# Splitting 512-column TensorE products into two of 256 in six dense stages of a hybrid block, with shifted weight tiles, seven more start-up products and two more K buffers

## Chip, cores and metric

The kernel runs on one core of a Trainium2 chip. The metric is the device time of one execution in microseconds; three executions of the kernel before the change are shown with their median. The engines have short names: PE is TensorE (matrix products), PEld its weight loads, DVE is VectorE, ACT is ScalarE, POOL is GpSimd, SP is SyncE, which here issues transfers.

## What is computed

One layer of a streaming encoder on 512 tokens of width 1024, in fp32. Two token mixers run side by side on one input projection and are gated and added, then come cross-attention into a memory of 256 rows and a gated FFN with a short convolution. Cut to what matters here:

```python
h = rms_norm(x, norm_mix_g)
proj = h @ w_in + b_in                    # 1024 -> 4864: stage "in"
y_a = rwkv7_branch(proj[..., :cb0], ...) @ w_branch_a          # stage "ya"
y_b = rglru_branch(proj[..., cb0:cb1], proj[..., cb1:cb2], ...) @ w_branch_b   # "yb"
merged = sigmoid(proj[..., cb2:cg1]) * y_a + sigmoid(proj[..., cg1:]) * y_b
x = x + merged @ w_mix_out                # "mix"
# cross-attention: keys and values of the memory, "k" and "v"
q = rms_norm(x, norm_x_g) @ w_cq          # "q"
x = x + attention(q, mem @ w_ckv) @ w_co  # "co"
x = x + conv_ffn(rms_norm(x, norm_ffn_g), w_ffn_in, ..., w_ffn_out)
return rms_norm(x, norm_final_g)
# rwkv7_branch: S_t = S_{t-1} diag(w_t) + (S_{t-1} a_t) b_t^T + v_t k_t^T, y_t = S_t r_t
```

## The kernel before

Activations are held transposed: 128 channels on the partitions, the 512 tokens along the free dimension. A dense stage goes through its output in blocks of 128 channels; each block is one accumulator `ps` of 128 x 512 in PSUM, and its sum runs over blocks of 128 input channels.

Every fp32 operand is split into a high and a low half of a shorter type (fp32r), and a product of fp32 matrices is three products of halves: `mm3` makes high by high (L179), high weight by low activation (L180) and low weight by high activation (L181). `dense` (L201 to L209) calls `mm3` for each input block and takes the weights from a `Units` object, which streams them from HBM: SP loads 128 x 1024 of raw weights (512 KB, L112), ACT casts them to the high half (L122), DVE subtracts for the low half (L123). The high half lies in a tile that `weight_tiles` allots; its argument `at` says how many elements from the tile's start the data begins. OFF is 32 elements, 128 bytes. Before the change the K, V and FFN stages pass OFF, the six stages named in, yb, ya, mix, q and co pass nothing and start at 0. K and FFN products have 256 columns, those of the six stages 512. An optional `nsum` lets `dense` put small products of a running sum (`sum_behind`) behind one of its own.

The stages run in this order. First `wake`: NWAKE products of constants (L300) on PE while the first weights arrive. Then the K stage: eight accumulators `k_ps` of 256 columns, each scaled by DVE into a tile `kt` (L360) and stored by POOL to the scratch `dK` (L361); `kt` has six buffers. Then V (`v_ps`), then the input projection: 38 blocks `in_ps`, in an order written out at the head of the file: 12, 13, 4, 5, 0, 1, 8, 9, 6, 7, 2, 3, 10, 11 and then 22 to 37, 14 to 21. Each block is 8 input blocks by 3 products. Its result is scaled by ACT and mixed with the token before by DVE (L597, L598); these make `pr` (r), `pk` (k) and `vT` (v) of the delta-rule branch, whose four pairs of heads, 0 to 3, are prepared while the projection goes on. For a pair i, PE makes two small products `psw` and `psa` (L620, L621), a sum of squares `ss`, and 16 small products `sc` (L691, from `AK` and `KBt`); DVE makes `KBt` from `kk` and `pk` (L653, L654) and evacuates `sc` into `AK` and `BZ` (L696, L697), ACT copies parts of `BZ` (L698). Of all pairs, SP stores a matrix (`dM`) and loads it again in another layout (`Nm`); on it DVE runs a serial chain of 32 steps (`zz` and `Zt`, L763 and L764), copied to `Zn`. The recurrence over chunks follows (products `zh`, `zo` and others) amid the last blocks of the projection, then yb, ya, mix, q with the attention, co, the FFN and the output.

What sets the order: each engine runs its instructions in one fixed order and waits at each for semaphores of other engines. The order is made by the tile framework's scheduler when the kernel is built, from priorities, dependences and its own costs; a change of the number or the size of instructions so moves others, too. Buffers of a tile name are used in turn, and an instruction that writes a buffer waits for the readers of what lay in it before: `in_ps` blocks so wait for the DVE instruction that read an earlier block.

Of the kernel before, what the change touches and what calls it, by code (L numbers as in the profile page):

```python
# [9 lines left out]
F32 = mybir.dt.float32  # L10
# [7 lines left out]
P = 128  # L18
T = 512
D = 1024  # L20
KB = D // P
NMEM = 256
# [11 lines left out]
NMID = 10  # L34
NWAKE = 11
KNORM = 5
# [22 lines left out]
def hybrid_block_kernel(ctx: ExitStack, tc: tile.TileContext, xT_d, mT_d, pv_d, cst_d, win_d, wk_d, wv_d,  # L59
# [39 lines left out]
    OFF = 32  # L99
# [78 lines left out]
    def mm3(ps, lh, ll, rh, rl, start, stop, **kw):  # L178
        first = PE.matmul(ps, lh, rh, start=start, stop=False, **kw)  # L179
        PE.matmul(ps, lh, rl, start=False, stop=False, **kw)  # L180
        PE.matmul(ps, ll, rh, start=False, stop=stop, **kw)  # L181
        return first
# [18 lines left out]
    def dense(ps, units, rhs, nkb, nsum=0):  # L201

        for kb in range(nkb):
            wh, wl = units.next()
            rh, rl = rhs(kb)
            ins = mm3(ps, wh, wl, rh, rl, kb == 0, kb == nkb - 1)
            if kb * nsum % nkb < nsum:
                sum_behind(ins)
        return ins  # L209
# [85 lines left out]
    with tc.tile_pool(name="p0", bufs=1, reuse_waits="tile") as p0:  # L295
# [6 lines left out]
        o = PV["nmem"][0]  # L302
# [55 lines left out]
        def k_out(m):  # L358
            kt = p0.tile([P, NMEM], F32, tag="kt", name=f"kt{m}", bufs=6)
            ins = V.tensor_tensor(kt, k_ps[m], rm, ALU.mult)  # L360
            nc.gpsimd.dma_start(dK[m], kt)  # L361
            return ins
# [36 lines left out]
        for hf in range(2):  # L399
            pss = [(mm_ps if hf else rw_ps)(f"v_ps{hf}_{i}") for i in range(2)]  # L400
            for k2 in range(4):
                wh, wl = next(st)
                for kk in range(2):
                    kb = 2 * k2 + kk
                    rh, rl = wh[:, kk * T:(kk + 1) * T], wl[:, kk * T:(kk + 1) * T]
# [170 lines left out]
    for i in range(2):  # L576
        with tc.issue_after(wdma[-1].ins):
            nc.sync.dma_start(lraw[i], lup_d[i])
    uin = Units(win_d, "win")
    last_in = None  # L580
# [131 lines left out]
    for jp in range(2):  # L712
# [10 lines left out]
        for j in js:  # L723
# [3 lines left out]
            at, L, Pp = prep(j)  # L727
# [22 lines left out]
    with tc.tile_pool(name="pz", bufs=1, reuse_waits="tile") as pz:  # L750
# [9 lines left out]
        for s in range(30, -1, -1):  # L760
            n = 31 - s
# [245 lines left out]
    for b in range(4):  # L1007
        yb = YB[:, b, :]
        with tc.high_priority():
            S.copy(yb2[:, 0, b, :], yb)  # L1010
            V.tensor_tensor(yb2[:, 1, b, :], yb, yb2[:, 0, b, :].bitcast(F32), ALU.subtract)
    ub = Units(wbb_d, "wbb")
    for m in range(KB):
# [11 lines left out]
    pm = pm_ctx.enter_context(tc.tile_pool(name="pm", bufs=2, reuse_waits="tile"))  # L1025
    ua = Units(wba_d, "wba")
    for m in range(KB):
# [25 lines left out]

    um = Units(wmix_d, "wmix")
    for m in range(KB):
        xin = pm.tile([P, T], F32, tag="xin", name=f"xin{m}")
        nc.scalar.dma_start(xin, xT_d[:, m, :])
        ps = mm_ps(f"mix_ps{m}")
# [57 lines left out]
    vs = vs[1:] + load_kv("V", 1)  # L1116
    uq = Units(wq_d, "wq")

# [78 lines left out]
    order = [0, 4, 1, 5, 2, 6, 3, 7]  # L1197
    uo = Units(wo_d, "wo", order)
    for m in order:
        ps = mm_ps(f"co_ps{m}")  # L1200
# [367 lines left out]
```

## Time and profile before

| | |
|---|---|
| time, median of three (lowest, highest) | 880.66 us (880.45, 881.25) |
| the profiled execution's own time | 880.43 us |
| its span, first to last instruction | 878.6 us |
| mean granted clock of TensorE | 0.997 |
| in_ps7, first and last product start | 108.02, 113.28 us |
| in_ps22, first product start | 147.21 us |
| in_ps14, first product start | 245.53 us |
| yb, first product start | 345.41 us |

The span is what the profile covers; the metric has 1.8 us more. Starts are counted from the span's first instruction. In the profile's rows numbers of buffers are left out, so `in_ps` stands for all 38 blocks; which one a row belongs to follows from its place in the order above, 24 products to a block. The duration printed for a product includes its way through the array, and products overlap: the distance between two starts is what one costs.

### The profile page before, as it was taken

What the parts mean: (1) busy time and instruction counts of PE and PEld (TensorE: products, weight loads), DVE (VectorE), ACT (ScalarE), POOL (GpSimd) and SP (SyncE); (2) the same over time, 40 slices, a digit from 0 to 9 for tenths busy, and PEclk for the clock granted to TensorE, in tenths of its full rate; (3) what the DMA queues carried; (4) which work ended last, traced back from release to release, by engine and by line L of the source; (5) the groups of instructions that cost most, each with busy time, mean ns of one, the idle gap of its engine ahead of it and who ended that gap; (6) DMA issues with size and microseconds to landing.
All of it is one profiled execution on the core that took longest, in us unless ns stands there. A gap on an engine that the chain in (4) does not pass through costs nothing.

```text
span 878.6 us, 15940 instructions
## 1 busy us (share of the span) xinstructions
PE 864.2 (98%) x6197; PEld 754.2 (86%) x6197; DVE 676.5 (77%) x1096; ACT 514.6 (59%) x788; POOL 132.6 (15%) x163
## 2 busy tenths in 40 slices
PE   8999999999999999999999999999999999999996
PEld 7778878888877677888887778999999999999996
DVE  6796598777976776785565568799888888999774
ACT  7576676634437576334454456666666566867563
POOL 0102222021101022001112211102111111111100
PEclk9999999999999999999999999999999999999998
DMA  8978899768996369758887868999999999898963
GB/s 285 307 249 219 206 224 235 190 186 257 264 230 160 86 167 249 197 185 222 226 237 174 203 155 192 251 272 266 307 262 262 320 279 303 253 293 206 300 193 96
DMA packets 97562, 201.37 MB, mean 229 GB/s; under 512 B 19600, under 2 KB 30992, under 8 KB 97424
## 3 DMA queue, kind: packets, MB, share of 16 engines
q1 hardware_dynamic: 62240, 118.57, 40.6%
q0 software_dynamic: 25504, 67.38, 37.4%
q10 hardware_dynamic: 9744, 14.42, 5.0%
q8 instruction: 48, 0.79, 0.4%
q14 instruction: 26, 0.21, 0.1%
HBM read 188.54 MB, written 78.12 MB: 303 GB/s over the span
## 4 chain that ended last, share of the span: by engine, by line
PE 89%; DVE 6%; ACT 2%; DMA 2%; issue 1%; DVEq 0%; ACTq 0%; SPq 0%
PE in_ps L180 7%; PE in_ps L179 7%; PE in_ps L181 7%; PE fx_ps L179 4%; PE fx_ps L181 4%; PE fx_ps L180 4%; PE fyz_ps L181 3%; PE fyz_ps L179 3%; PE fyz_ps L180 3%; PE ox_ps L179 2%; PE ox_ps L181 2%; PE ox_ps L180 2%; PE oyz_ps L179 2%; PE oyz_ps L181 2%; PE oyz_ps L180 2%; PE q_ps L180 2%
## 5 line engine op out<-in xcount | busy, mean ns | idle before, releaser
L145 ACT CAST wfi_h<-wfi_r 128x1024 fp32r<-128x1024 f32 x77 | 80.9, 1051 | 69.7 <-PE fyz_ps L180 24.7
L180 PE MATMUL in_ps<-hT,win_h 128*128 128x512 f32 x304 | 120.9, 398 | 0.4 <-DVE hT L396 0.4
L181 PE MATMUL in_ps<-hT,win_l 128*128 128x512 f32 x304 | 121.2, 399 | 0.0
L179 PE MATMUL in_ps<-hT,win_h 128*128 128x512 f32 x304 | 120.8, 399 | 0.3 <-DVE pr L598 0.3
L494 POOL DMA_DIRECT2D dS<-in_wfi x66 | 66.8, 1028 | 296.9 <-PE in_ps L179 106.5
L146 DVE TENSOR_TENSOR wfi_l<-wfi_r,wfi_h 128x1024 fp32r<-128x1024 f32 x77 | 94.0, 1220 | 22.5 <-ACT wfi_h L145 22.4
L180 PEld LDWEIGHTS in_ps<-hT,win_h 128*128 128x128 f32 x304 | 57.1, 188 | 14.4 <-DVE hT L396 1.0
L179 PEld LDWEIGHTS in_ps<-hT,win_h 128*128 128x128 f32 x304 | 57.1, 188 | 13.3 <-DVE pr L598 0.7
L181 PEld LDWEIGHTS in_ps<-hT,win_l 128*128 128x128 f32 x304 | 57.1, 188 | 13.3 <-issue 0.7
L530 POOL DMA_DIRECT2D dOs<-in_wfo x54 | 39.8, 801 | 168.3 <-PE fx_ps L179 43.2
L123 DVE TENSOR_TENSOR win_l<-win_r,win_h 128x1024 fp32r<-128x1024 f32 x38 | 46.3, 1220 | 24.6 <-ACT win_h L122 23.9
L122 ACT CAST win_h<-win_r 128x1024 fp32r<-128x1024 f32 x38 | 39.9, 1050 | 42.1 <-PE in_ps L180 37.7
L1379 DVE TENSOR_TENSOR wfo_l<-wfo_r,wfo_h 128x1024 fp32r<-128x1024 f32 (+1 forms) x39 | 47.0, 1208 | 11.2 <-ACT wfo_h L1378 11.2
L1378 ACT CAST wfo_h<-wfo_r 128x1024 fp32r<-128x1024 f32 (+1 forms) x39 | 40.4, 1036 | 24.5 <-DMA wfo_r<-dOs 10.4
L181 PE MATMUL fyz_ps<-hq,wfi_l 128*128 128x256 f32 x176 | 48.7, 277 | 0.4 <-DVE wfi_l L146 0.4
L179 PE MATMUL fyz_ps<-hq,wfi_h 128*128 128x256 f32 x176 | 48.8, 277 | 0.1
L179 PE MATMUL fx_ps<-hr,wfi_h 128*128 128x256 f32 x176 | 48.7, 277 | 0.0
L179 PE MATMUL fx_ps<-hq,wfi_h 128*128 128x256 f32 x176 | 48.6, 276 | 0.0
L180 PE MATMUL fx_ps<-hq,wfi_h 128*128 128x256 f32 x176 | 48.6, 276 | 0.0
L181 PE MATMUL fx_ps<-hq,wfi_l 128*128 128x256 f32 x176 | 48.6, 276 | 0.0
L180 PE MATMUL fyz_ps<-hq,wfi_h 128*128 128x256 f32 x176 | 48.6, 276 | 0.0
L181 PE MATMUL ox_ps<-go,wfo_l 128*128 128x256 f32 x176 | 48.6, 276 | 0.0
(432 smaller groups left out, 2689.8 us busy)
## 6 DMA issues: line engine op xcount, KB each, us to landing
dS<-in_wfi POOLq DMA_DIRECT2D x66, 512.0 KB, 7.9
wfi_r<-dS SPq DMA_DIRECT2D x44, 512.0 KB, 7.0
win_r<-in_win SPq DMA_DIRECT2D x38, 512.0 KB, 5.3
wfi_r<-in_wfi SPq DMA_DIRECT2D x33, 512.0 KB, 6.5
dS<-dS POOLq DMA_DIRECT2D x22, 512.0 KB, 5.6
dOs<-in_wfo POOLq DMA_DIRECT2D x12, 512.0 KB, 8.5
wk_r<-in_wk SPq DMA_DIRECT2D x8, 512.0 KB, 5.0
wv_r<-in_wv SPq DMA_DIRECT2D x8, 512.0 KB, 5.0
```

What stands on the lines that cost most here:

```text
L122: casts.append(S.copy(hi[:, o:o + n], raw[:, o:o + n]))
L123: V.tensor_tensor(lo[:, o:o + n], raw[:, o:o + n], hi[:, o:o + n].bitcast(F32), ALU.subtract)
L145: S.copy(hi, raw)
L146: V.tensor_tensor(lo, raw, hi.bitcast(F32), ALU.subtract)
L179: first = PE.matmul(ps, lh, rh, start=start, stop=False, **kw)
L180: PE.matmul(ps, lh, rl, start=False, stop=False, **kw)
L181: PE.matmul(ps, ll, rh, start=False, stop=stop, **kw)
L494: return lambda: nc.gpsimd.dma_start(s(out), src, **kw)
L530: yield lambda k=k, w=w, src=src: nc.gpsimd.dma_start(dO[n, m][:, k * P:(k + w) * P], src, **kw)
L1378: S.copy(hi[:, :n], raw[:, :n])
L1379: V.tensor_tensor(lo[:, :n], raw[:, :n], hi[:, :n].bitcast(F32), ALU.subtract)
```

## The change

`dense` makes each of its products in pieces of at most 256 columns, half of T: for each input block it first makes the three products of the left half, then the three of the right half, into the two halves of the same accumulator, with `start` on the very first only. For K, whose accumulators have 256 columns, nothing changes. The six stages pass `at=OFF`. NWAKE goes from 11 to 18, and `kt` gets eight buffers. Lines behind L203 stand three lower in the changed file.

```diff
-NWAKE = 11
+NWAKE = 18
...
     def dense(ps, units, rhs, nkb, nsum=0):
 
+        n = min(ps.shape[-1], T // 2)
         for kb in range(nkb):
             wh, wl = units.next()
             rh, rl = rhs(kb)
-            ins = mm3(ps, wh, wl, rh, rl, kb == 0, kb == nkb - 1)
+            for o in range(0, ps.shape[-1], n):
+                ins = mm3(ps[:, o:o + n], wh, wl, rh[:, o:o + n], rl[:, o:o + n],
+                          kb == 0 and o == 0, kb == nkb - 1, skip_group_check=o > 0)
             if kb * nsum % nkb < nsum:
                 sum_behind(ins)
         return ins
...
-            kt = p0.tile([P, NMEM], F32, tag="kt", name=f"kt{m}", bufs=6)
+            kt = p0.tile([P, NMEM], F32, tag="kt", name=f"kt{m}", bufs=8)
...
-    uin = Units(win_d, "win")
+    uin = Units(win_d, "win", at=OFF)
...
-    ub = Units(wbb_d, "wbb")
+    ub = Units(wbb_d, "wbb", at=OFF)
...
-    ua = Units(wba_d, "wba")
+    ua = Units(wba_d, "wba", at=OFF)
...
-    um = Units(wmix_d, "wmix")
+    um = Units(wmix_d, "wmix", at=OFF)
...
-    uq = Units(wq_d, "wq")
+    uq = Units(wq_d, "wq", at=OFF)
...
-    uo = Units(wo_d, "wo", order)
+    uo = Units(wo_d, "wo", order, at=OFF)
```

The scheduler makes another order of it. Three places are shown; numbers behind names tell tiles apart, and the first number in `sc1`, `psw2` or `win_l14` is that of the pair of heads or of the weight load.

The first place is on PE, around the small products `sc1` of the second pair of heads, about 131 to 139 us in the profile. Before, thirteen of the products of in_ps10 stand ahead of them (the last two of these are the first rows here), and others between them:

```order
L181 MATMUL in_ps10_1395<-hT2_0_87,win_l12_1399 128x512
L179 MATMUL in_ps10_1395<-hT2_0_87,win_h12_1398 128x512
L691 MATMUL sc1_0_0_1205<-AK_753,KBt_751 128x128 x4
L180 MATMUL in_ps10_1395<-hT2_1_88,win_h12_1398 128x512
L181 MATMUL in_ps10_1395<-hT2_0_87,win_l12_1399 128x512
L691 MATMUL sc1_0_1_1206<-AK_753,KBt_751 128x128 x4
L691 MATMUL sc1_1_0_1221<-AK_753,KBt_751 128x128
L691 MATMUL sc1_1_1_1222<-AK_753,KBt_751 128x128
```

In the changed program, on the same engine, the last product of in_ps3 comes straight before `sc1`, and in_ps10 behind it:

```order
L181 MATMUL in_ps3_1629<-hT2_0_87,win_l11_1633 128x256
L694 MATMUL sc1_0_0_1404<-AK_760,KBt_758 128x128 x4
L694 MATMUL sc1_0_1_1405<-AK_760,KBt_758 128x128 x4
L694 MATMUL sc1_1_0_1420<-AK_760,KBt_758 128x128
L694 MATMUL sc1_1_1_1421<-AK_760,KBt_758 128x128
...
L623 MATMUL psw2_1812<-pwa0_845,lhi_777 128x512
L624 MATMUL psw2_1812<-pwa0_845,llo0_778 128x512
L623 MATMUL psa2_1813<-pwa1_846,lhi_777 128x512
L624 MATMUL psa2_1813<-pwa1_846,llo1_779 128x512
L179 MATMUL in_ps10_1690<-hT2_0_87,win_h12_1693 128x256
```

All of in_ps10 moved behind `sc1`, and `psw2` and `psa2` moved from behind in_ps11 to ahead of in_ps10.

The second place is on DVE at the same time of the program. Before, `pr2` (which reads in_ps2) stands ahead of the `KBt` instructions, and `pk3` (which reads in_ps7) amid the evacuations of `sc1`:

```order
L598 SCALAR_TENSOR_TENSOR pr2_1319<-in_ps2_1320,dp_679,q2_1353 128x512
L653 TENSOR_TENSOR KBt_751<-kk1_1180,L1_1168 64x8x64
L650 TENSOR_TENSOR pk1_899<-pk1_899,at1_1171 128x512
L123 TENSOR_TENSOR win_l14_1554<-win_r14_1551,win_h14_1553 128x1024
L654 TENSOR_TENSOR KBt_751<-pk1_899,L1_1168 64x8x64
...
L697 TENSOR_TENSOR BZ_750<-sc1_0_1_1206,cst_76 64x4x64
L598 SCALAR_TENSOR_TENSOR pk3_1281<-in_ps7_1282,dp_679,q7_1315 128x512
L696 TENSOR_TENSOR AK_753<-sc1_1_0_1221,cst_76 64x512
```

In the changed program, on DVE:

```order
L657 TENSOR_TENSOR KBt_758<-pk1_978,L1_1367 64x8x64
L664 SCALAR_TENSOR_TENSOR pr1_1100<-pr1_1100,pv_75,pk1_978 128x512
L123 TENSOR_TENSOR win_l14_1897<-win_r14_1894,win_h14_1896 128x1024
L699 TENSOR_TENSOR AK_760<-sc1_0_0_1404,cst_76 64x512
L700 TENSOR_TENSOR BZ_757<-sc1_0_0_1404,cst_76 64x4x64
...
L699 TENSOR_TENSOR AK_760<-sc1_1_1_1421,cst_76 64x512
L700 TENSOR_TENSOR BZ_757<-sc1_1_1_1421,cst_76 64x4x64
L601 SCALAR_TENSOR_TENSOR pk3_1504<-in_ps7_1505,dp_686,q7_1562 128x512
L601 SCALAR_TENSOR_TENSOR pr2_1566<-in_ps2_1567,dp_686,q2_1624 128x512
```

`pk3` and `pr2` moved behind all four evacuations of `sc1`, and `win_l14` behind `KBt`. In the built program in_ps10 waits for `pr2` before the change and for `pk3` after it, since its accumulator is another one.

The third place is on DVE at the end of the serial chain on `Zt`, about 242 to 249 us. Before:

```order
L763 TENSOR_TENSOR zz_2039<-Zt_2037,Nm_2036 128x900
L123 TENSOR_TENSOR win_l30_3088<-win_r30_3085,win_h30_3087 128x1024
L764 TENSOR_REDUCE Zt_2037<-zz_2039 128x30
L763 TENSOR_TENSOR zz_2039<-Zt_2037,Nm_2036 128x961
L764 TENSOR_REDUCE Zt_2037<-zz_2039 128x31
L765 COPY Zn_2038<-Zt_2037 128x1024
```

In the changed program, on DVE:

```order
L123 TENSOR_TENSOR win_l29_3756<-win_r29_3753,win_h29_3755 128x1024
L767 TENSOR_REDUCE Zt_2620<-zz_2622 128x30
L766 TENSOR_TENSOR zz_2622<-Zt_2620,Nm_2619 128x961
L767 TENSOR_REDUCE Zt_2620<-zz_2622 128x31
L768 COPY Zn_2621<-Zt_2620 128x1024
L123 TENSOR_TENSOR win_l30_3815<-win_r30_3812,win_h30_3814 128x1024
```

`win_l30`, the low half of the weights of in_ps14, moved from ahead of the last steps to behind the chain and the copy; `win_l29` stands where it stood.

## The prediction

> **What bounds the kernel now.** Read first: the page's head, with each engine's busy time, and the chain of work that ended last.
> ```profile
> span 878.6 us, 15940 instructions
> ...
> PE 864.2 (98%) x6197; PEld 754.2 (86%) x6197; DVE 676.5 (77%) x1096; ACT 514.6 (59%) x788; POOL 132.6 (15%) x163
> ...
> PE 89%; DVE 6%; ACT 2%; DMA 2%; issue 1%; DVEq 0%; ACTq 0%; SPq 0%
> ```
> TensorE (PE) is busy for 98% of the span and carries 89% of the chain. So two things set the time: the pace at which products follow one another, and the moments in which PE waits. The list of PE's waits comes next. Its first two rows are:
> ```profile
> PE k_ps L179 <- ACT wk_h L122: 1.5, 1, 1.5
> PE k_ps L179 <- DVE kt L360: 1.1, 1, 1.1
> ```
> All its rows together make 7 us, so little is to be gained there, and much can be lost by an order that makes PE wait more.
>
> The pace can't be read from the durations in the groups:
> ```profile
> L181 PE MATMUL in_ps<-hT,win_l 128*128 128x512 f32 x304 | 121.2, 399 | 0.0
> L179 PE MATMUL fyz_ps<-hq,wfi_h 128*128 128x256 f32 x176 | 48.8, 277 | 0.1
> ```
> Two of 277 ns would be more than one of 399, but products overlap (304 of 399 in each of three lines, and all else, would not fit into the span). What counts is the distance between starts, in the timeline of PE (start, duration, engine, line, operation):
> ```profile
> 394.78 0.39 PE L179 MATMUL mix_ps<-mg,wmix_h 128*128 128x512 f32 x1
> ...
> 404.39 0.39 PE L179 MATMUL mix_ps<-mg,wmix_h 128*128 128x512 f32 x1
> 125.27 0.39 PE L179 MATMUL in_ps<-hT,win_h 128*128 128x512 f32 x1
> ...
> 130.54 0.39 PE L181 MATMUL in_ps<-hT,win_l 128*128 128x512 f32 x1
> 568.23 0.28 PE L179 MATMUL fyz_ps<-hr,wfi_h 128*128 128x256 f32 x1
> ...
> 571.97 0.28 PE L179 MATMUL fx_ps<-hr,wfi_h 128*128 128x256 f32 x1
> ```
> The first pair lies 42 products apart: 9.61/42 = 228.8 ns. The second, the 24 products of one block of the input stage: 5.27/23 = 229.1 ns. The last pair, in the FFN, where products have 256 columns, 33: 3.74/33 = 113.3 ns, that is 226.7 for two.
>
> **The change, part by part.** (1) *Two products of 256 for one of 512.* The input stage has 3 x 304 products, q, mix and co 3 x 64 each, yb and ya 3 x 32 each:
> ```profile
> L179 PE MATMUL q_ps<-hx,wq_h 128*128 128x512 f32 x64 | 25.5, 398 | 0.0
> L180 PE MATMUL yb_ps<-yb,wbb_h 128*128 128x512 f32 x32 | 12.7, 395 | 0.4 <-DVE yb L1011 0.4
> ```
> Together 912 + 576 + 192 = 1680. At the FFN's pace each pair saves 229.1 - 226.7 = 2.4 ns: 1680 x 2.4 = 4.0 us. 1680 more weight loads come with it; the FFN does one per 113 ns too, so they hide there.
>
> Against this stands a rule of the Trainium skill ("TensorE: Matmul & The Clock Gate", section "Wait — 56ns, not 53.3ns?"): each product costs its columns at 2.4 GHz plus a fixed 2.5 ns. By it two halves take 218.3 ns and one whole 215.8, so the split would lose 1680 x 2.5 = 4.2 us instead of winning. The trace disagrees on both ends (113.3 and 228.8), and there the half is a little less than half; I take the rows.
>
> (2) *High weights 128 bytes further on.* No row shows it alone in these stages. The nearest is the V stage, whose high weights already lie there and whose products have 512 columns:
> ```profile
> 37.54 0.39 PE L180 MATMUL v_ps<-wv_l,m 128*128 128x512 f32 x1
> ...
> 39.61 0.40 PE L180 MATMUL v_ps<-wv_l,m 128*128 128x512 f32 x1
> 41.13 0.38 PE L179 MATMUL k_ps<-m,wk_h 128*128 128x256 f32 x1 [1.12 <-DVE kt L360]
> ```
> 9 products in 2.07 us are 230 ns: the place alone does nothing visible, so it counts at 0 here, between the whole 4.0 and none of it; the FFN has width and place together.
>
> (3) *Eight buffers for K.* The last row above starts 1.52 us after its forerunner; at 0.23 that is 1.3 us lost. VectorE (DVE) shows why:
> ```profile
> 40.65 0.42 DVE L360 TENSOR_TENSOR kt<-k_ps,rm 128x256 f32<-128x256 f32 x1 [1.89 <-DMA dK<-kt]
> ```
> It waits for a store of K to free one of six buffers. With eight for eight tiles there is no such wait. DVE's next work then comes 1.9 earlier, but PE can gain only what it lost: -1.3 us, between 0 (the next weights aren't ready either) and -1.9.
>
> (4) *Eighteen constant products.*
> ```profile
> 1.07 5.06 PE L300 MATMUL wake<-onesr 128*128 128x512 f32 x11 [1.07 <-DVE Pp L628]
> 7.64 0.39 PE L179 MATMUL k_ps<-m,wk_h 128*128 128x256 f32 x1 [1.51 <-ACT wk_h L122]
> ```
> The eleven take 5.06/11 = 0.46 us each and end at 6.1; six more stand before the first K product and one behind it. At the pace of 0.23 that products of this width have later they take 1.4 us and end inside the idle 1.51: 0. At the slow pace 6 x 0.46 = 2.8 would end at 8.9: +1.3. I take 0: the idle covers six at up to 1.51/6 = 0.25 us.
>
> (5) *The order.* PE's program moves, and this is the largest term. In the changed program all of in_ps3 runs before sc1, and psw2, psa2 and in_ps10 come behind it; in_ps10 waits for DVE's `pk3` (it frees the accumulator of in_ps7), which now stands behind all evacuations of sc1. Before, in_ps10 waited for `pr2`, and PE did 13 of its 24 products before sc1:
> ```profile
> 131.22 0.51 PE L179 MATMUL in_ps<-hT,win_h 128*128 128x512 f32 x1 [0.29 <-DVE pr L598]
> 134.41 1.16 PE L691 MATMUL sc<-AK,KBt 64*128 64x128 f32 x8
> 136.16 2.05 PE L691 MATMUL sc<-AK,KBt 64*128 64x128 f32 x24
> 147.21 0.39 PE L179 MATMUL in_ps<-hT,win_h 128*128 128x512 f32 x1
> ```
> DVE sets the pace here; its rows in the same stretch:
> ```profile
> 130.42 0.74 DVE L598 SCALAR_TENSOR_TENSOR pr<-in_ps,dp,q 128x512 f32<-128x512 f32 x1
> 131.08 0.67 DVE L653 TENSOR_TENSOR KBt<-kk,L 64x512 f32<-64x512 f32 x1
> ...
> 132.32 1.22 DVE L123 TENSOR_TENSOR win_l<-win_r,win_h 128x1024 fp32r<-128x1024 f32 x1
> 133.46 0.68 DVE L654 TENSOR_TENSOR KBt<-pk,L 64x512 f32<-64x512 f32 x1
> 134.78 0.69 DVE L654 TENSOR_TENSOR KBt<-pk,L 64x512 f32<-64x512 f32 x1
> 135.61 0.69 DVE L696 TENSOR_TENSOR AK<-sc,cst 64x512 f32<-64x512 f32 x1
> 136.31 0.42 DVE L697 TENSOR_TENSOR BZ<-sc,cst 64x256 f32<-64x256 f32 x1
> 136.66 0.73 DVE L661 SCALAR_TENSOR_TENSOR pr<-pr,pv,pk 128x512 f32<-128x512 f32 x1
> 138.51 0.75 DVE L598 SCALAR_TENSOR_TENSOR pk<-in_ps,dp,q 128x512 f32<-128x512 f32 x1
> ```
> The first pk-half of KBt is there at 134.14. In the changed order `pr2` (0.66 to the next start) and win_l14 (1.14) go behind it, and the chain comes 1.8 earlier (1.3 of K, some 0.5 of faster products): 134.14 - 1.8 - 1.8 = 130.5; its second half 1.3 later, 131.9. Then `pr1` 0.7 and win_l14 1.14 (133.7), four pairs AK and BZ of 0.70 + 0.35 (137.9), `pk3` 0.75: in_ps10 starts at 138.7. in_ps10 and in_ps11 are 96 products of 113 ns (10.9), and ss2 and the restart take 0.5: in_ps22 starts at 150.1, against 147.21 before, +2.9. In between PE has only sc1's 3 us and psw2 and psa2 to do. DVE's chain may start 0.7 earlier or later, so PE waits some 4 to 5.5 us more there than before; by the earlier end I take +2.7 in all up to in_ps22, which holds the 1.3 of K and the 0.8 of that part's 336 products. Its lower end, were none of the waits there, is -2.1.
>
> The same order comes back for sc2 (now inside in_ps23, before behind it) and sc3: PE reaches the last KBt some 0.5 us too early each time: +0.9 (0 to 2).
>
> (6) *The Z chain.* The weight half win_l30, which in_ps14 needs for its third product, stands behind all 32 steps of DVE's Z chain and the copy Zn, where before it stood ahead of the last:
> ```profile
> 188.25 3.19 SPq L703 DMA_DIRECT2D dM<-BZ  x4
> 197.72 1.86 SPq L757 DMA_DIRECT2D Nm<-dM  x2
> 204.95 0.16 DVE L763 TENSOR_TENSOR zz<-Zt,Nm 128x1 f32<-128x1 f32 x1 [3.60 <-DMA Nm<-dM]
> 242.74 1.22 DVE L123 TENSOR_TENSOR win_l<-win_r,win_h 128x1024 fp32r<-128x1024 f32 x1
> 247.39 1.12 DVE L765 COPY Zn<-Zt 128x1024 f32<-128x1024 f32 x1
> 245.99 0.39 PE L181 MATMUL in_ps<-hT,win_l 128*128 128x512 f32 x1
> ```
> The chain starts when Nm lands. From there win_l30 is ready after 247.39 - 204.95 - 1.14 + 1.04 + 1.22 = 43.6 us, at 248.5 if the start stays. PE comes at 245.99 + 2.7 + 0.9 - 1.0 (its faster products on the way) = 248.6. So each us by which the chain starts later is a us of PE. dM's stores follow sc3, which comes a little later; Nm's load stands before a weight load on SP's queue instead of behind one. I take 1 us (0 to 4): +1.0.
>
> (7) *The rest.* The other 1344 products give 1344 x 2.4 = -3.2. In the recurrence fewer changes between kinds of products (about -0.3); the FFN's order is the same.
>
> **Sum**, against the profiled execution's own 880.43 us (1.8 more than its span, and 0.2 under the 880.66 of the median): +2.7 + 0.9 + 1.0 - 3.2 - 0.3 = +1.1, so **881.5 us**: a gain of 5.3 in pace and buffers that PE's new waits take back. By the Trainium skill's rule of (1), which is C at its dearest, it would be 8.2 more, 889.7.
>
> **Rivals.** *A: the waits of (5) and (6) hardly come*, because DVE and ScalarE, which also start earlier, reach KBt and pk3 before PE does. For it: DVE waited here for little, so its order could close up. Against: DVE's rows of (5) stand one behind the other without a gap, so they move up only by what is taken from them. 880.43 - 5.3 and 0.3 of waits left: 875.4.
> *B: the Z chain starts late.* If dM's stores come as late as PE at sc3 (2.7 + 0.9) and Nm follows, the chain starts 4 us late instead of 1, and PE stands before win_l30 for 3 us more: 884.5. It decides from a start of the chain at 206 on: below that B costs nothing more than forecast. For it: the stores follow sc3's evacuations. Against: sc3 stands earlier in in_ps27 than PE's delay.
> *C: the split brings no pace*, because not the width costs the 2.4 ns but what these stages read, or because each product carries a cost of its own that two halves pay twice: then the 4.0 us are missing, 885.5, and more the larger that cost. For it: wide products differ by stage, 228.8 to 230, so something beside the columns counts. Against: the FFN's 113.3 is under half of each of them.
>
> **Chances.** Forecast 0.40 (own range 878 to 883.5), A 0.34, B 0.17, C 0.09. 0.2% is 1.8 us, about what a measurement can tell from no change: 878.9 to 882.4. Faster: A 0.33 + 0.04 of the forecast = 0.37. Same: 0.23 + 0.01 of A + 0.01 of B = 0.25. Slower: 0.13 + 0.16 of B + 0.09 of C = 0.38. The range runs from 874.8 (A with all of the pace) to 885.0 (B and a little over).
>
> **What would show it.** Right: starts 113 ns apart in in_ps and mix; no wait at kt; a wait of over 1 us before in_ps10 put down to `pk`, more at sc and psw; in_ps22 near 150; a wait for win_l at in_ps14. Wrong: in_ps22 near 145 (A), the first zz past 208 (B), 115 ns or more in in_ps (C).

## The result, and the profile after

| | before | changed |
|---|---|---|
| time, median (lowest, highest) | 881.34 us (880.45, 881.74), 6 runs | 901.21 us (900.06, 906.4), 6 runs |
| the profiled execution's own time | 880.43 | 900.06 |
| its span | 878.6 | 898.3 |
| in_ps22, first product start | 147.21 | 153.56 |
| in_ps14, first product start | 245.53 | 252.07 |
| yb, first product start | 345.41 | 356.35 |
| ya, first product start | 368.69 | 385.89 |
| q, first product start | 434.60 | 451.66 |
| FFN, first product start | 552.55 | 572.41 |
| output projection, first product start | 764.07 | 783.72 |

The ratio is 1.0236, 95% interval 1.0219 to 1.0254: the change makes the kernel 19.9 us **slower**. The prediction said 881.5 with a range of 874.8 to 885.0.

The table says where. The loss comes in four pieces, each in a place where a stage gives way to something else: +6.35 up to in_ps22, hardly anything (+0.2) between in_ps22 and in_ps14, +4.4 from there to yb, +6.3 inside yb, nothing in ya and mix (-0.1), +2.8 from q to the FFN, and nothing behind that (-0.2).

The page of the changed kernel (the span; busy time of each engine, its share and its instructions):

```profile
span 898.3 us, 19307 instructions
PE 870.4 (97%) x7884; PEld 836.2 (93%) x7884; DVE 678.6 (76%) x1096; ACT 514.9 (57%) x788; POOL 133.0 (15%) x163
```

PE is still busy for 97% of the span, so the share alone does not show the loss; it counts products that run slowly as busy too. PE's waits show more (engine, line, tile, what it waited for: us in total, times, longest):

```profile
PE yb_ps L179 <- DVE mB L1021: 3.7, 1, 3.7
PE sc L694 <- DVE KBt L657: 2.9, 5, 0.9
PE yb_ps L179 <- ACT ge L268: 1.5, 1, 1.5
PE psw L623 <- ACT BZ L701: 1.4, 1, 1.4
PE gv L176 <- DVE gv_l L174: 1.4, 2, 0.8
PE v_ps L180 <- DVE wv_l L123: 1.3, 2, 0.8
...
PE psa L623 <- ACT L L268: 0.8, 1, 0.8
PE in_ps L179 <- DVE pk L601: 0.7, 1, 0.7
```

All rows of this view together make 20.4 us, against 7.2 before: +13.2. Nearly every name that is new stands where the order has changed: psw, psa and `pk` around in_ps10, gv, ge and mB around the end of the recurrence and yb. Of the five waits for `KBt` two of 0.2 us stand ahead of sc1, the others ahead of sc0 (0.9), sc2 and sc3 (0.8 each). The wait for `kt` is gone, and the one for `wv_l` has grown from 0.8 to 1.3.

PE's timeline around the first of these places (start, duration, operation, wait ahead of it):

```profile
132.94 2.02 PE L694 MATMUL sc<-AK,KBt 64*128 64x128 f32 x24 [0.20 <-DVE KBt L657]
136.38 0.50 PE L623 MATMUL psw<-pwa,lhi 128*128 128x512 f32 x1 [1.42 <-ACT BZ L701]
...
137.89 0.79 PE L623 MATMUL psa<-pwa,lhi 128*128 128x512 f32 x1 [0.78 <-ACT L L268]
...
139.83 0.58 PE L179 MATMUL in_ps<-hT,win_h 128*128 128x256 f32 x1 [0.72 <-DVE pk L601]
140.21 0.41 PE L180 MATMUL in_ps<-hT,win_h 128*128 128x256 f32 x1
...
144.26 0.41 PE L181 MATMUL in_ps<-hT,win_l 128*128 128x256 f32 x1
```

in_ps10 starts at 139.83, after three waits in a row. DVE's rows show what it waited for: `pk3` comes behind the last evacuations of `sc1`, one row after the other.

```profile
130.80 0.68 DVE L657 TENSOR_TENSOR KBt<-pk,L 64x512 f32<-64x512 f32 x1
...
138.56 0.43 DVE L700 TENSOR_TENSOR BZ<-sc,cst 64x256 f32<-64x256 f32 x1
139.02 0.75 DVE L601 SCALAR_TENSOR_TENSOR pk<-in_ps,dp,q 128x512 f32<-128x512 f32 x1
```

And then the 20 products from 140.21 to 144.26 start (144.26 - 140.21)/19 = 213 ns apart instead of 113: they run at half speed. The view of stretches shows what halved (stretch, its length, PE busy and its instructions, granted clock, DMA share, GB/s), here and in yb:

```profile
135.00:136.00 1.00, 0.00 (x0) 1.00 0.81 217
143.00:144.00 1.00, 1.00 (x6) 0.50 0.99 56
371.00:372.00 1.00, 0.00 (x0) 1.00 1.13 139
374.00:375.00 1.00, 1.00 (x6) 0.50 0.81 133
```

The granted clock is 1.00 while PE stands still, then falls to 0.50 for some 6.8 us in the first place (137.9 to 144.7) and 3.4 us in the second, with 6 or 7 products in a stretch of a microsecond instead of 11 (the view counts those that reach into it, too). The Trainium skill ("TensorE: Matmul & The Clock Gate", section "What's actually happening") has such a gate: half clock after an idle window of about 3.4 us, full clock after about as long under load. In yb the trace agrees, with 3.4 us at 0.50 behind a wait of 3.7; in the first place the halving did not need one idle stretch of that length, since the waits before it were 1.42 and 0.78 us.

The second place, yb. First PE's two products around its longest wait, then DVE's rows in the same stretch:

```profile
369.30 0.28 PE L181 MATMUL yb_ps<-yb,wbb_l 128*128 128x256 f32 x1
373.28 0.45 PE L179 MATMUL yb_ps<-yb,wbb_h 128*128 128x256 f32 x1 [3.70 <-DVE mB L1021]
```

```profile
369.51 0.68 DVE L939 TENSOR_TENSOR vT<-y,gg 128x512 f32<-128x512 f32 x1
370.11 0.69 DVE L945 TENSOR_TENSOR ya<-vT,ya 128x512 fp32r<-128x512 f32 x1
370.71 1.22 DVE L123 TENSOR_TENSOR wba_l<-wba_r,wba_h 128x1024 fp32r<-128x1024 f32 x1
371.84 0.69 DVE L945 TENSOR_TENSOR ya<-vT,ya 128x512 fp32r<-128x512 f32 x1
372.44 1.88 DVE L1021 TENSOR_TENSOR mB<-yb_ps,gb 128x512 f32<-128x512 f32 x3
```

DVE is never idle here. It finishes the recurrence's outputs (vT, ya, and y ahead of them) and a weight half for the next stage, and only then reads yb's accumulators out, three at once; PE waits until the first of them is free. In the trace of before `mB` stands between the same kinds of rows, one at a time:

```profile
357.02 0.68 DVE L1018 TENSOR_TENSOR mB<-yb_ps,gb 128x512 f32<-128x512 f32 x1
357.62 0.68 DVE L936 TENSOR_TENSOR vT<-y,gg 128x512 f32<-128x512 f32 x1
358.21 0.68 DVE L1018 TENSOR_TENSOR mB<-yb_ps,gb 128x512 f32<-128x512 f32 x1
```

When yb starts, DVE has 11 rows of the recurrence's outputs (y, gv_l, vT, ya) before it in the old order and 14 in the changed one, and 12 of these 14 stand between the first `mB` and the second. No run shows why the scheduler puts them so.

The 4.4 us between in_ps14 and yb lie ahead of this. The last input products fill PE while the recurrence's chain of small products (from the first `vr` to the last `y`) waits on other engines. One of the three rows of in_ps between the chain's last product and yb, before and then changed (count: shortest, median, longest duration in ns, first and last start):

```profile
L180 PE MATMUL in_ps<-hT,win_h x21: 388/394/502, 326.7 to 342.8; 128*128 128x512 f32 x21
```

```profile
L180 PE MATMUL in_ps<-hT,win_h x67: 276/276/682, 322.5 to 351.9; 128*128 128x256 f32 x67
```

With their sisters these are 62 products of 512 columns (31,744) before, and 200 of 256 (51,200) now. The chain takes fewer with it (47 of 512 before, 55 of 256 now) and runs 47.2 us instead of 53.0; what it leaves stands behind it, 34.0 us up to yb instead of 18.9. Ahead of the chain it is the other way round: it starts 23.1 us after in_ps14 instead of 28.0. The products themselves are only moved by this. What is new in the stretch are PE's waits (for BZ, UV, xb, gv_h, gv_l and ge): 4.1 us instead of 0.3, 3.8 of the 4.4. No experiment took these waits away by themselves.

### The profile page after: what moved, and what is told of

Its sections match the earlier page's. It is cut to its first block, busy times and chain, and to the rows that moved or that the text cites. A ratio compares the mean times of both kernels' runs of the same rounds, so it can differ in the third digit from the quotient of the medians.

```text
span 898.3 us, 19307 instructions
## 1 busy us (share of the span) xinstructions
PE 870.4 (97%) x7884; PEld 836.2 (93%) x7884; DVE 678.6 (76%) x1096; ACT 514.9 (57%) x788; POOL 133.0 (15%) x163
## 3 DMA queue, kind: packets, MB, share of 16 engines
q8 instruction: 62, 1.02, 0.5%
## 4 chain that ended last, share of the span: by engine, by line
PE 54%; DVE 5%; ACT 2%; issue 1%; DMA 1%; DVEq 0%; ACTq 0%
PE fx_ps L181 4%; PE fx_ps L179 4%; PE fx_ps L180 4%; PE fyz_ps L181 3%; PE fyz_ps L180 3%; PE fyz_ps L179 3%; PE ox_ps L181 2%; PE ox_ps L179 2%; PE ox_ps L180 2%; PE oyz_ps L181 2%; PE oyz_ps L179 2%; PE oyz_ps L180 2%; PE co_ps L179 2%; PE co_ps L181 2%; PE co_ps L180 2%; PE mix_ps L180 1%
## 5 line engine op out<-in xcount | busy, mean ns | idle before, releaser
L180 PE MATMUL in_ps<-hT,win_h 128*128 128x256 f32 x608 | 171.3, 282 | 0.5 <-DVE hT L399 0.5
L179 PE MATMUL in_ps<-hT,win_h 128*128 128x256 f32 x608 | 170.1, 280 | 0.7 <-DVE pk L601 0.7
L181 PE MATMUL in_ps<-hT,win_l 128*128 128x256 f32 x608 | 170.1, 280 | 0.0
L179 PEld LDWEIGHTS in_ps<-hT,win_h 128*128 128x128 f32 x608 | 115.2, 190 | 2.7 <-DVE pk L601 1.4
L180 PEld LDWEIGHTS in_ps<-hT,win_h 128*128 128x128 f32 x608 | 115.3, 190 | 2.5 <-DVE hT L399 0.7
L181 PEld LDWEIGHTS in_ps<-hT,win_l 128*128 128x128 f32 x608 | 115.2, 190 | 1.1 <-issue 0.7
L146 DVE TENSOR_TENSOR wfi_l<-wfi_r,wfi_h 128x1024 fp32r<-128x1024 f32 x77 | 94.2, 1223 | 19.9 <-ACT wfi_h L145 19.9
L1382 DVE TENSOR_TENSOR wfo_l<-wfo_r,wfo_h 128x1024 fp32r<-128x1024 f32 (+1 forms) x39 | 47.4, 1218 | 11.2 <-ACT wfo_h L1381 11.0
L179 PE MATMUL fx_ps<-hr,wfi_h 128*128 128x256 f32 x176 | 48.7, 277 | 0.0
L180 PE MATMUL fx_ps<-hr,wfi_h 128*128 128x256 f32 x176 | 48.6, 276 | 0.0
L181 PE MATMUL fx_ps<-hr,wfi_l 128*128 128x256 f32 x176 | 48.6, 276 | 0.0
L179 PE MATMUL fx_ps<-hq,wfi_h 128*128 128x256 f32 x176 | 48.6, 276 | 0.0
```

Of the source, the lines that this page charges most:

```text
L146: V.tensor_tensor(lo, raw, hi.bitcast(F32), ALU.subtract)
L1382: V.tensor_tensor(lo[:, :n], raw[:, :n], hi[:, :n].bitcast(F32), ALU.subtract)
```

## The experiments

Each kernel was timed against the kernel before on the same chip. All the diffs are against the changed kernel where nothing else is said, and the times are medians.

### Which part of the change loses the time

Four kernels take it apart. *split_only*: the halves in all six stages, nothing else of the change.

```diff
-NWAKE = 18
+NWAKE = 11
-            kt = p0.tile([P, NMEM], F32, tag="kt", name=f"kt{m}", bufs=8)
+            kt = p0.tile([P, NMEM], F32, tag="kt", name=f"kt{m}", bufs=6)
-    uin = Units(win_d, "win", at=OFF)
+    uin = Units(win_d, "win")
...
-    uo = Units(wo_d, "wo", order, at=OFF)
+    uo = Units(wo_d, "wo", order)
```

> The halves in all six stages, with the weights at their old place, 11 start-up products and six K buffers. Theory O (the loss comes from the order that the halves bring, through PE's waits and the half clock after them): 899 to 903 us, as the whole change. Rival P (the loss comes from the shifted weights, the K buffers or the start-up products): 877 to 881. If O holds, starts 113 to 114 ns apart in ya and mix would show that the pace needs the width alone and not the place.

Measured: 910.97 us, ratio 1.0332 (1.0316 to 1.0349). Slower even than the whole change by some 9 us, which no theory expected. The FFN starts at 582.34 instead of 572.41. Its timeline of PE in mix shows the pace, against the changed kernel in ya:

```profile
418.03 0.28 PE L179 MATMUL mix_ps<-mg,wmix_h 128*128 128x256 f32 x1
...
421.92 0.28 PE L179 MATMUL mix_ps<-mg,wmix_h 128*128 128x256 f32 x1
```

```profile
390.31 0.28 PE L179 MATMUL ya_ps<-ya,wba_h 128*128 128x256 f32 x1
...
393.71 0.28 PE L179 MATMUL ya_ps<-ya,wba_h 128*128 128x256 f32 x1
```

33 products in 3.89 us are 117.9 ns each; 30 in 3.40 us are 113.3. So in mix halves reach the FFN's pace only with the high weights 128 bytes further on (an exception in co follows under "Place and width"). At 4.5 ns for each of the halves that run slowly this is some 14 us, more than the loss against the changed kernel; where the rest came back stays open.

*in_only*: halves and place in the input stage alone.

```diff
-        n = min(ps.shape[-1], T // 2)
+        n = min(ps.shape[-1], T // 2) if units.name == "win" else ps.shape[-1]
```

(yb, ya, mix, q, co without `at=OFF`, NWAKE 11, `kt` 6.)

> Halves and shifted weights in the input stage alone; yb, ya, mix, q and co as before, K buffers and start-up products as before. Theory O: the whole loss up to the start of ya is here (some 17 us of the 20), so 896 to 900 us, with the long waits before psw2, in_ps10 and in yb and two stretches at half clock. Rival R (the loss is spread over all stages, since halves are dearer wherever small products stand between them): 886 to 891.

Measured: 899.36, ratio 1.0187 (1.0162 to 1.0211), within theory O. The input stage's halves alone cost 17 of the 20 us: yb starts at 363.85 in the profiled execution, the FFN at 573.15. But they do not cost them in the same places. The waits before psw2, psa2 and in_ps10 and the half clock behind them are those of the changed kernel; in yb PE waits 0.8 us for `mB` instead of 3.7, and no half clock follows. In their place stands another row, which the changed kernel does not have:

```profile
PE in_ps L181 <- DVE win_l L123: 3.8, 6, 0.8
```

These six waits lie between 216 and 254 us, where DVE runs the chain on `Zt`. Its first `zz` starts at 216.05 here and at 206.46 in the changed kernel, and in_ps14 at 259.46 instead of 252.07. That the two totals lie so near each other is in part luck.

*late_only*: the reverse, halves and place in the other five stages (`units.name != "win"`, `uin` without `at=OFF`, NWAKE 11, `kt` 6).

> Halves and shifted weights in yb, ya, mix, q and co alone; the input stage, K buffers and start-up products as before, so that the order up to yb is that of before. Theory O: no long waits; the pace gains 768 x 2.4 ns = 1.8 us, the attention's new order with 12 more changes between products takes some 1 to 4 us (in the whole change q to co took 2.7 us longer): 880 to 884 us. Rival R: 889 or more. If the pace were all that counts: 879.5.

Measured: 883.71, ratio 1.0024 (1.0016 to 1.0033). That is within theory O. PE's order up to yb is that of before, there is no half clock behind the first K products, and no wait for `mB`. From the first q product to the FFN it takes 120.84 us (556.69 - 435.85) against 117.95 before, although the products alone should gain: the +2.8 of q to the FFN come from here.

*rest_only*: the place, eighteen constant products and eight buffers, but whole products.

```diff
-            for o in range(0, ps.shape[-1], n):
-                ins = mm3(ps[:, o:o + n], wh, wl, rh[:, o:o + n], rl[:, o:o + n],
-                          kb == 0 and o == 0, kb == nkb - 1, skip_group_check=o > 0)
+            ins = mm3(ps, wh, wl, rh, rl, kb == 0, kb == nkb - 1)
```

> Shifted weights in all six stages, 18 start-up products and eight K buffers, but whole products of 512 columns. Theory O: 879.5 to 881.3 us: the K wait gives up to 1.3, the place nothing, starts in ya and mix still 226 to 232 ns apart. Rival P: slower than 890, or, if the place alone makes the pace, 876 to 878 with 226.7 ns.

Measured: 884.39, ratio 1.0031 (1.002 to 1.0041), where a small gain was expected. PE in ya:

```profile
373.90 0.39 PE L179 MATMUL ya_ps<-ya,wba_h 128*128 128x512 f32 x1
...
380.87 0.39 PE L179 MATMUL ya_ps<-ya,wba_h 128*128 128x512 f32 x1
```

30 products in 6.97 us are 232.3 ns, against 228.8 before. The same 128 bytes that halves need slow whole products down.

### Is it the order?

The theory now was that the input stage's halves lose their time through the order that the scheduler makes around them. *evac_first* keeps the changed kernel and gives the two instructions that read an input block's accumulator out a higher priority, so that `pk3` no longer stands behind sc1's evacuations.

```diff
-        S.activation(q[:, 1:T], ps[:, 0:T - 1], AF.Identity, scale=par("mu", blk), bias=par("b_in", blk))
-        V.scalar_tensor_tensor(out, ps, omu[:, blk:blk + 1], q, ALU.mult, ALU.add)
+        with tc.high_priority():
+            S.activation(q[:, 1:T], ps[:, 0:T - 1], AF.Identity, scale=par("mu", blk), bias=par("b_in", blk))
+            V.scalar_tensor_tensor(out, ps, omu[:, blk:blk + 1], q, ALU.mult, ALU.add)
```

> The whole change, with the two instructions that read an in_ps block for r, k and v (ACT's and DVE's) given a higher priority, so that pk3 and pr2 stand ahead of the evacuations of sc1 and part of in_ps10 ahead of sc1 again. Theory O: the waits before psw2, psa2 and in_ps10 (3 us) and the half clock behind them (some 2.5 us) go, in_ps22 starts 4 to 6 us earlier; 895 to 898 us against 901.2. Rival W (DVE has too much work there, the wait only moves): in_ps22 stays past 152 and the time past 899.

Measured: 899.28, ratio 1.0206 (1.019 to 1.0222). A miss by 1.3 us in the total, where rival W's "past 899" holds, but its place behaves as theory O says. The stretch in which the changed kernel waits and runs at 0.50, and in_ps22's first product:

```profile
138.00:140.00 2.00, 2.00 (x19) 1.00 1.00 170
```

```profile
147.86 0.28 PE L179 MATMUL in_ps<-hT,win_h 128*128 128x256 f32 x1
```

None of the three waits, no half clock, and in_ps22 starts at 147.86 instead of 153.56: 5.7 of the 6.35 are back. But in_ps14 starts at 249.14, 2.9 before the changed kernel's: half of the gain is given back on the way, and of the total only some 2 us are left. Two waits for a `win_l` (0.6 us each) stand on this way that the changed kernel does not have: PE comes earlier, and DVE's chain on `Zt` hardly does (its first `zz` starts at 205.70, against 206.46). The wait of 3.7 us for `mB` and the half clock behind it stay.

*evac_mb* gives `mB` the same priority in addition.

```diff
-        V.tensor_tensor(mB[:, m, :], psb, gb, ALU.mult)
+        with tc.high_priority():
+            V.tensor_tensor(mB[:, m, :], psb, gb, ALU.mult)
```

> As evac_first, and DVE's product mB, which frees the yb accumulators, with a higher priority too. Theory O: the wait of 3.7 us of PE in yb and the half clock behind it (1.7 us) go: 890 to 893 us. Rival W: PE then waits as long for ya, whose halves DVE makes later: 895 to 898.

Measured: 895.45, ratio 1.0166 (1.0147 to 1.0185), in rival W's range and not in theory O's. yb behaves as theory O says: the wait for `mB` and the half clock are gone, and it takes 24.05 us (353.61 to 377.66) instead of 29.54, against 23.28 before. But mix takes 47.4 (399.42 to 446.84) instead of 44.0. One row of PE's waits, three stretches and a row of DVE at the start of ya say why:

```profile
PE mix_ps L179 <- ACT mg L1039: 1.4, 1, 1.4
```

```profile
405.00:406.00 1.00, 0.26 (x1) 1.00 0.58 180
407.00:408.00 1.00, 1.00 (x7) 0.50 0.05 21
410.00:411.00 1.00, 1.00 (x10) 0.95 0.95 162
```

```profile
382.81 0.69 DVE L1037 TENSOR_TENSOR gta<-ya_ps,gta 128x512 f32<-128x512 f32 x1 [2.76 <-DMA gta<-dG]
```

PE waits 1.4 us in mix, a further 0.3 one product on, and then runs at half clock for 3.4 us. It waits for `mg`, which DVE and ACT make from ya's accumulators and the gates `gta`. DVE starts with these 5.2 us after ya's first product instead of 2.9, since the first load of `gta` takes 7.3 us here (issued at 375.47) and 4.2 in the changed kernel. So the gain in yb came back in part as a wait in another place, this time behind a transfer, and the wait brought its own half clock along.

*prep_whole* leaves the scheduler alone and changes its input: of the input stage's 38 blocks the twelve around sc1, sc2 and sc3 are whole again, at place 0 (`dense` is given a flag, and `at` a function of the block).

```diff
-    uin = Units(win_d, "win", at=OFF)
+    WHOLE = (6, 7, 2, 3, 10, 11, 22, 23, 24, 25, 26, 27)
+    uin = Units(win_d, "win", at=lambda g: 0 if IN_ORDER[g] in WHOLE else OFF)
...
-        last_in = dense(ps, uin, lambda kb: (h2[:, 0, kb, :], h2[:, 1, kb, :]), KB, NSUM.get(i, 0))
+        last_in = dense(ps, uin, lambda kb: (h2[:, 0, kb, :], h2[:, 1, kb, :]), KB, NSUM.get(i, 0), i in WHOLE)
```

> The whole change, but with the twelve input blocks 6, 7, 2, 3, 10, 11 and 22 to 27, among which the heads' pairs are prepared, whole and their weights at the old place; so the order there is that of before, and behind in_ps14 nearly that of the change. Theory O: in_ps22 starts within 1 us of before's 147.2; the recurrence and yb still lose 4 to 10 us, q to co 2.7: 886 to 893 us. Rival S (all the loss behind in_ps14 comes from being late at sc1): 879 to 883.

Measured: 890.82, ratio 1.0104 (1.0088 to 1.0119), half of the loss and within theory O; in_ps22 starts at 146.84. The recurrence's chain takes 48.9 us with 17,920 input columns, and 46,592 are left for the 30.7 us behind it: between the two kernels in both. yb takes 24.1 (351.92 to 376.02) and has no long wait. What is left over before's time stands between in_ps14 and yb (+5.4) and from q to the FFN (+2.8), and smaller parts between in_ps22 and in_ps14 (+1.4, with 1.7 of waits for `win_l`) and in yb (+0.8).

### Place and width

Two kernels, each run once, give each stage another place: yb 64 bytes, ya 32, mix 256, q 384, co 512. *place_half* does it in late_only, where these stages have halves; this diff is against late_only.

```diff
-    ub = Units(wbb_d, "wbb", at=OFF)
+    ub = Units(wbb_d, "wbb", at=16)
-    ua = Units(wba_d, "wba", at=OFF)
+    ua = Units(wba_d, "wba", at=8)
-    um = Units(wmix_d, "wmix", at=OFF)
+    um = Units(wmix_d, "wmix", at=64)
-    uq = Units(wq_d, "wq", at=OFF)
+    uq = Units(wq_d, "wq", at=96)
-    uo = Units(wo_d, "wo", order, at=OFF)
+    uo = Units(wo_d, "wo", order, at=128)
```

(`at` counts elements of 4 bytes.)

> Halves in yb, ya, mix, q and co alone, as in late_only, but the high weights at five places: yb 64 bytes on, ya 32, mix 256, q 384, co 512. At 0 bytes a half took 117.8 ns, at 128 bytes 113.3. Theory any (only place 0 is bad): 113.3 in all five. Theory period (what counts is the place within 256 or 512 bytes): mix and co, or co alone, at 117.8, the others 113 to 116. One time of 882 to 885 us.

Measured: 889.05, one time, 4 us or more above what was expected. PE in mix (256 bytes) and in q (384 bytes):

```profile
399.97 0.28 PE L179 MATMUL mix_ps<-mg,wmix_h 128*128 128x256 f32 x1
...
403.86 0.28 PE L179 MATMUL mix_ps<-mg,wmix_h 128*128 128x256 f32 x1
...
443.90 0.28 PE L179 MATMUL q_ps<-hx,wq_h 128*128 128x256 f32 x1
...
444.92 0.28 PE L179 MATMUL q_ps<-hx,wq_h 128*128 128x256 f32 x1
```

3.89/33 = 117.9 ns at 256 bytes, 1.02/9 = 113.3 at 384. co at 512 bytes has 117.8, yb and ya at 64 and 32 bytes 118 and 119 in the mean. So of the places tried 128 and 384 give the fast pace, and the others do not. The four slow stages have 1152 halves; at 4.5 ns each they cost 5.2 us, which is the distance from late_only's 883.71. *place_whole* has the same places in the kernel before, with whole products.

> The kernel before with the high weights of the five later stages at the same five places, products whole. At 0 bytes a whole product took 228.8 ns, at 128 bytes 231.8. Theory any: 231.8 in all five; theory period: 228.8 in mix and co, or in co alone. One time of 880 to 885 us.

Measured: 880.98, one time. The mean distance of starts over the three products of a step (lines 179, 180, 181) is 232 ns in q at 384 bytes, as at 128 in rest_only; 229 in mix at 256 and 230 in co at 512, as at 0; 231 in yb at 64 and 232 in ya at 32. So width and place depend on each other: of the places tried, whole products are fastest at 0, 256 and 512 and halves at 128 and 384; 32 and 64 are slow for both.

One thing does not fit. In split_only, at place 0, co ran at 117.8 in the first thirteen of its 64 steps of six products (one of them at 113.3), and at 113.3 in the 51 from 547.7 us to its end; one input block ran at 113.4, too. The slow pace at place 0 is thus no constant, and the place alone does not set it; what does stays open.

### The start

*wake_only* is the kernel before with NWAKE 18 instead of 11; *wake_kt* has eight `kt` buffers in addition.

> The kernel before with 18 start-up products and nothing else. In the profiled executions of in_only, late_only and split_only, with eleven, 15 to 25 products of the K stage start 213 ns apart; with 18, and in the one execution that the prediction read, none. Theory K (whether the K stage starts at half pace differs between executions with eleven): 880.0 to 881.2 us, the slow half of before's times (882 and more) gone. Rival Z (the start-up products change nothing): 881.5 to 882.5, as before.

> The kernel before with 18 start-up products and eight K buffers. If PE gets the 1.3 us that it waits for kt: 1.3 us under wake_only, 879.5 to 880.0. If another wait takes its place (in the changed kernel PE waited 0.5 us more for the V weights' low half): 880.5 to 881.2, as wake_only, with in_ps starting at 55.5 to 56.

Measured: 881.08, ratio 0.9991 (0.9982 to 1.0000), and 881.06, ratio 0.9991 (0.9982 to 1.0), against 881.67 before on either chip. Both intervals reach to 1, so a gain is not shown, though the values lie in theory K's range, and none of wake_only's eleven runs is over 882 where six of before's twenty are. The buffers bring nothing that these times show. In wake_kt's waits the row for `kt` is gone, and the one for `wv_l` is longer than before:

```profile
PE v_ps L180 <- DVE wv_l L123: 1.3, 2, 0.8
```

In wake_only's profiled execution the row for `kt` is missing too, with six buffers, while the six others with six buffers have it; so this pair does not show what the buffers do.

What the constant products may bring lies at the first K products. In late_only, with eleven, two starts are 0.21 us apart; in wake_only, with eighteen, 0.12:

```profile
9.04 0.41 PE L181 MATMUL k_ps<-m,wk_l 128*128 128x256 f32 x1
9.25 0.41 PE L179 MATMUL k_ps<-m,wk_h 128*128 128x256 f32 x1
```

```profile
9.30 0.28 PE L180 MATMUL k_ps<-m,wk_h 128*128 128x256 f32 x1
9.42 0.28 PE L181 MATMUL k_ps<-m,wk_l 128*128 128x256 f32 x1
```

Some 25 products run so in that execution of late_only, 2.5 us. In split_only's execution such a stretch stands in the view with half the clock:

```profile
10.00:11.00 1.00, 1.00 (x6) 0.50 1.07 415
```

No profiled execution with eighteen has such a stretch. Before's own profiled execution had none either, so this is a matter of the single execution, and in the mean worth at most the 0.6 us above.

### Halves in fewer places

*best1* has halves and place only in the input stage's first eight blocks, yb, ya and mix. The other thirty blocks, q and co are whole at place 0 (`whole` and the function for `at` are those of prep_whole, with the thirty blocks in WHOLE).

```diff
-        n = min(ps.shape[-1], T // 2)
+        n = ps.shape[-1] if whole or units.name in ("wq", "wo") else min(ps.shape[-1], T // 2)
...
-    uq = Units(wq_d, "wq", at=OFF)
+    uq = Units(wq_d, "wq")
...
-    uo = Units(wo_d, "wo", order, at=OFF)
+    uo = Units(wo_d, "wo", order)
```

> Halves with shifted weights only where no small products stand between: the first eight input blocks, yb, ya and mix (192 + 384 products); the other 30 input blocks, q and co whole with their weights at the old place; 18 start-up products, eight K buffers. Its order is that of before but for a few rows. Theory O: 576 x 2.3 ns = 1.3 us of pace, 1.3 of K's buffers, and about 1 in the mean from the start-up products, against the 882.0 of this chip's runs of before: 877.5 to 879.5. If halves cost more than they give even there: 881 or more.

Measured: 880.08 (879.33 to 880.88, 11 runs), ratio 0.9981 (0.9972 to 0.9990), 0.6 us above what was expected. yb starts at 344.98, and q to the FFN takes 117.74. It is the one kernel here whose interval lies below 1, by 1.6 us in the medians, of which wake_only alone has 0.6. That the split makes the other 1.0 is not shown. Its 576 split products should give 576 x 2.4 = 1.4 us, but from the first product of in_ps to the first of the output projection its profiled execution takes 707.9 us, wake_only's 707.5 and before's 707.7. Of the three split stages yb takes 23.60 us (before 23.28), ya 21.77 (21.97) and mix 44.05 (43.94). Behind that, wake_only's profiled execution has a wait of 0.8 us for `wfo_l` that the other two do not have.

## Why the prediction was wrong

*The step that failed most is (7), "the rest".* It costed everything behind in_ps14 at the pace of the products and -0.3 for fewer changes in the recurrence. There lie +4.4 up to yb, +6.3 in yb and +2.8 from q on, two thirds of the loss. The changed order was read at in_ps10, sc2, sc3 and the Z chain only; that the chain would now run with 55 halves inside it instead of 47 whole products, and what DVE would then have to do in yb, was no term of it, though the order of both programs was there to read. In place of it the runs show waits: 3.8 us more between in_ps14 and yb, 3.9 more inside yb (3.7 of it for `mB`) with 1.6 of half clock behind them, which evac_mb takes away, and the 2.8 from q on, which late_only has by itself.

*(5), the order at sc1,* had the right mechanism and too small a size: +2.7 up to in_ps22 were predicted, 6.35 measured. in_ps10 came at 139.83 where 138.7 was worked out. The chain of DVE's rows ran as said, but from 131.48 on, where `KBt`'s first pk-half was there, instead of 130.5: the start "1.8 earlier" was only 0.9, since the 1.3 of K did not come and PE waited 0.9 ahead of sc0. The larger part is what the sum had no term for: 21 products 100 ns slower each at half clock, 2.1 us, beside some 0.5 in psa. evac_first shows that they hang on the wait: without it they are gone. The +0.9 at sc2 and sc3 was right in kind and within its range: PE waits 0.83 and 0.76 us there for `KBt`, and not at all before.

*(6), the Z chain,* was +1.0 and is nothing: from in_ps22 to in_ps14 the two kernels differ by 0.2, and PE's waits have no row for win_l at in_ps14. The chain did start later, at 206.46 instead of 204.95, and win_l30 came behind it at 249.01; but PE reached in_ps14 at 252.07 instead of some 248.6 and so had nothing to wait for. Rival B did not come in this kernel, but its mechanism shows elsewhere: in in_only and split_only the first `zz` starts at 216.05 and 215.33, and PE waits 3.8 and 1.2 us for `win_l`. A did not come, whose in_ps22 near 145 stands against 153.56, nor C, since ya and mix run at 113.3. Of the signs named, the pace, the missing wait at `kt` and the longer waits at sc and psw came; the wait for `pk` is 0.7 us and not over 1, and in_ps22 is far from 150.

*(1) and (2)* have the right pace by luck. Where halves run undisturbed they take 113.3 ns, as said. But (2) put the place at 0 and the whole 4.0 on the width. By place alone whole products lose (231.8 ns a product in the mean of ya's three lines, against 228.8), by width alone halves take 117.8 in mix, 235.6 for two; only both together gain 2.4, and the change happened to make both. The V stage, from which (2) took its value, has its weights where the other stages have the activations (`v_ps<-wv_l,m`), and did not answer for them. Nor did the 4.0 us come out whole: ya and mix, with 288 split products, are 0.14 us faster together instead of 0.7, with a new wait of 0.2 in mix. The Trainium skill's rule quoted in (1) ("TensorE: Matmul & The Clock Gate", section "Wait — 56ns, not 53.3ns?"), a fixed 2.5 ns for each product, holds for neither: 113.3 x 2 is less than 228.8, and at place 0 the loss is 6.8.

*(3), eight buffers,* was -1.3 and is nothing that the times show: 881.06 in wake_kt, 881.08 in wake_only. The text named the case (the next weights aren't ready either), and part of it came: the wait at `kt` went, the one for `wv_l` grew by 0.5. *(4)* was 0, and is between 0 and -0.6 beside before's median.

*Not seen at all* was the half clock, in the input stage and in yb, together 21 x 0.1 + 16 x 0.1 + 0.5 = 4.2 us; and that halves make each change to another kind of product dearer. From q to the FFN the changed order has 101 groups of products against 89, and the first sc product behind a half starts 74 ns later than the columns of q or co ahead of it need at 113.3 ns for 256, against 18 behind a whole one. That the narrow product hides less of what a change costs is argued from these distances; late_only shows only that the stretch with q and co loses with halves.

The account: waits +13.2, half clock +4.2, q to the FFN +2.6 beside the 0.2 of waits in it, pace of the other 1296 products -3.1 (worked out, not measured), together +16.9 of the 19.7 by which the output projection's start moved. The remaining 2.8 us were not placed; more changes between kinds of products in the recurrence are a candidate that no run priced.

## What to carry to other kernels

When an instruction is split, the scheduler's order behind it is a new program: compare the built order on every engine to the end of the kernel, and look for who is overtaken at each stage's boundary, before any saving per instruction is counted. A wait of PE can cost twice, once as the wait and again as several microseconds at half clock behind it, so a kernel whose PE is busy for 98% of the span loses more than its waits add up to. Width and place of operands are to be tried together, first where nothing else stands between the products, and what they bring is to be read in the stage's own stretch: a median that is 1 us lower can come from another place.

## What the runs showed that was not expected

A product's pace depends on where its weights lie as well as on its width. For 512 columns: 228.8 ns at place 0, 231.8 at 128 bytes; for 256 columns: 117.8 at 0, 256 and 512 bytes, 113.3 at 128 and 384, 118 to 119 at 64 and 32. That the place within 256 bytes is what counts is a guess that fits these stages but not split_only's co, which ran at 113.3 at place 0 for most of its length.

PE's clock can halve after short waits: two of 1.42 and 0.78 us, with two products between them, were followed by 6.8 us at 0.50, and in evac_mb two of 1.4 and 0.3, with one product between them, by 3.4. A single wait of 1.5 us for ge, ahead of yb, was not. At the program's start late_only's products stand 0.21 us apart in stretches whose granted clock reads 1.00, where split_only's column reads 0.50 at the same distance; so there the starts tell the pace, and the column need not.
